# RWKV-7 / mLSTM trunk on one core: small products alternate between partition groups, and the state chain moves into one PSUM bank

## The chip, the core and the metric

The kernel runs on one core of a Trainium2 chip. The metric is the device time of one execution in microseconds, the median of several runs; lower is better. Engines are named as in the profile: PE (TensorE, matmuls), PEld (its weight loads), DVE (VectorE), ACT (ScalarE), POOL (GpSimd) and SP (SyncE, which issues most transfers).

## The reference, cut to what matters

Two layers over 1024 tokens of width 1024. Layer 0 mixes tokens with RWKV-7 (16 heads of 64) and layer 1 with a chunkwise mLSTM (8 heads); each is followed by a SwiGLU. What the change touches is mostly the RWKV-7 recurrence, one state of 64 x 64 for each head:

```
def _rwkv7_step(state, inp):
    r_t, w_t, k_t, v_t, a_t, b_t = inp
    sa = jnp.einsum('bhvk,bhk->bhv', state, a_t)
    state = state * w_t[:, :, None, :] + sa[..., None] * b_t[:, :, None, :] + v_t[..., None] * k_t[:, :, None, :]
    y = jnp.einsum('bhvk,bhk->bhv', state, r_t)
    return state, y
...
    w_log = -jax.nn.softplus(-(w0 + jnp.tanh(wl) @ w2)) - 0.5
    decay = jnp.exp(-jnp.exp(w_log.astype(jnp.float32)))
    a = jax.nn.sigmoid(a0 + al @ a2)
```

In the mLSTM it touches the scores inside a chunk, `jnp.einsum('bhctd,bhcsd->bhcts', q, k)`.

## The kernel before, in words

Activations lie with features on partitions and tokens along the free axis, in two halves of 512 tokens. A dense product is done in three passes (`dense`): weight and activation are each split into a high and a low part of type fp32r, and high x high, high x low and low x high are summed in one PSUM bank. These are the 128x512 matmuls named dn. A product of plain f32 operands is one call in the source and two MATMUL rows in the trace, so 256 calls stand there as x512.

RWKV-7 is computed in chunks of 64 tokens. A *pair* is two heads on the 128 partitions and one half of the tokens: 8 head pairs x 2 halves = 16 pairs, each of 8 chunks. Four functions work on a pair:

- `rw_prep` makes the chunk operands KB and AR and the scores: for each of two groups u and each head h, four products of 64 partitions (KB by AR) go into the one bank "sc", and two DVE multiplications by masks (line 630) write SA and SR from it.
- `rw_inverse` inverts the unit triangular 64 x 64 blocks in SA, starting with 16 x 16 blocks on DVE; then two rounds of 16 x 16 products (32 calls each, ordered by partition group q of 32 and then by chunk c) and, for e = 0 and then e = 1, two rounds of 32 x 32 products of 8 calls each. All use the one bank "iv", and ACT copies the result between rounds (lines 704, 712, 725, 729).
- `rw_solve` applies the inverse to the values (two rounds of 16 calls of 64 x 64 in bank "px") and to the chunk operand AR (for e = 0 and then e = 1, 8 calls in bank "tr").
- `rw_chain` carries the state through the 8 chunks, so 128 steps in all. A step: the product p1 = AR x state (bank "c1"), DVE adds p1 to VU (line 788), two products KT x VU into p3 (bank "c2"), DVE updates the state from p3 (line 793). Two products SR x VU, issued after the state update, are added into the other half of p1, and ACT copies that to Ys (line 798).

`chunks` runs 19 rounds: in round i the chain of pair i-3, the solve of pair i-2, the inverse of pair i-1, the prep of pair i and the finish of pair i-3. Between them it draws dense products from `fillers` (projections of the second half, gate, then the output projection and the first part of the SwiGLU) up to a quota. A list scheduler then sets the final order on every engine from this order and from priorities (`ahead`), each engine runs its instructions in that order, and the framework puts waits between accesses of different engines to one bank of the same PSUM tile. `bank(tag)` hands out a bank by tag: "dn" has two, each other tag one. The 8 banks are dn (2), sc, iv, tr, px, c1 and c2.

`lora` (the two low-rank maps for decay and a) adds a second product of 64 partitions, `hi[0:64] @ tl[0:64]`, to a first one of 128 partitions over `st`, whose upper half holds the high and whose lower half the low part of the same weights. It runs twice for each half of the tokens, with 8 output tiles each: 16 such products in each half. `ml_prep` computes for each of the 8 blocks of the mLSTM and for two heads four score products of 64 partitions, one head after the other, in banks "sc" and "iv".

Of the kernel before, what the change touches and what calls it, by code (L numbers as in the profile page):

```python
# [129 lines left out]
class K:  # L130
# [297 lines left out]
    def lora(self, hf, arr, xs=None):  # L428


        nc, A = self.nc, self.A
        first, second, bias, seg, func = {"s": ("lw", "w2", "w0", 1, AF.Tanh), "a": ("la", "a2", "a0", 4, AF.Copy)}[arr]
        xs = xs or self.mixed(seg)
        ps = self.bank("dn")
        self.dense(ps, self.weights(A[first]), xs)
        yield 5
        t = self.t("tmp")
        nc.scalar.activation(t, ps, func)
        th, tl = self.a0()
        self.split(th, tl, t)  # L440
        raw, hi, st = self.wtiles(A[second])
        nc.scalar.activation(hi, raw, AF.Copy)
        nc.scalar.activation(st[0:64], raw[0:64], AF.Copy)
        nc.vector.tensor_tensor(st[64:128], raw[64:128], hi[64:128].bitcast(F32), SUB)
        for j in range(KT):
            c = slice(j * P, j * P + P)
            ps = self.bank("dn")
            self.mm(ps, st[:, c], th, start=True, stop=False)
            self.mm(ps, hi[0:64, c], tl[0:64], start=False, stop=True)
            self.spill(arr, j, hf, ps, AF.Sigmoid, bias=self.col(bias, j))  # L450
            if hf == 0 or j % 4 == 3:
                yield 2
# [120 lines left out]
    def rw_prep(self, j, hf):  # L573
# [47 lines left out]
        for u in range(2):  # L621
            for h in range(2):
                hs = slice(64 * h, 64 * h + 64)
                ps = self.bank("sc", [P, 4, P])
                for q in range(4):
                    self.mm(ps[:, q], KB[hs, 4 * u + q, :], AR[hs, 4 * u + q, :])
                for t, at, m in ((SA, True, strict), (SR, False, incl)):
                    o = t.rearrange("p e (u h) t -> p u e h t", h=2)[:, 2 * u:2 * u + 2, :, h, :]
                    with self.ahead("mask"):
                        nc.vector.tensor_tensor(o, slots(ps, at), m, MUL)  # L630
# [26 lines left out]
    def rw_inverse(self, S):  # L657
# [39 lines left out]
        for q in range(4):  # L697
            r, e = slice(32 * q, 32 * q + 16), 0 if q >= 2 else 1
            o = 32 * (q % 2) + 16
            for c in range(8):  # L700
# [5 lines left out]
        for q in range(4):  # L706
            r = slice(32 * q, 32 * q + 16)
            for c in range(8):
# [10 lines left out]
        for e in range(2):  # L719
            o = 0 if e else 64  # L720
            r0, r1 = slice(o, o + 32), slice(o + 32, o + 64)
            ps = self.bank("iv", [P, 8, 32])
            for c in range(8):
                self.mm(ps[r1, c, :], SA[r0, e, c, 32:64], XN[r0, c, :], tile_position=(o, o + 32))
            nc.scalar.activation(Y1[r1], ps[r1], AF.Copy)
            ps = self.bank("iv", [P, 8, 32])
            for c in range(8):
                self.mm(ps[r0, c, :], Y1[r1, c, :], XD[r1, c, :], tile_position=(o + 32, o))
            nc.scalar.activation(SA[r0, e, :, 32:64], ps[r0], AF.Copy)

    def rw_solve(self, S):
# [22 lines left out]
        for c in range(8):  # L754
            vr, ur = self.rows(c)
            for h in range(2):
                o = (c // 2) * P + 64 * h
                self.mm(ps[ur, o:o + 64], SA[vr, c % 2, 2 * (c // 2) + h, :], VU[vr, c, 64 * h:64 * h + 64])
        nc.scalar.activation(Z, ps.rearrange("p (u f) -> p u f", f=P), AF.Copy)
        ps = self.bank("px")  # L760
        for c in range(8):
            vr, ur = self.rows(c)
            for h in range(2):
                o = (c // 2) * P + 64 * h
                self.mm(ps[ur, o:o + 64], SA[ur, c % 2, 2 * (c // 2) + h, :], Z[ur, c // 2, 64 * h:64 * h + 64])
        p3 = ps.rearrange("p (u f) -> p u f", f=P)
        nc.scalar.activation(VU[64:128, 0::2, :], p3[64:128], AF.Copy)
        nc.scalar.activation(VU[0:64, 1::2, :], p3[0:64], AF.Copy)
        for e in range(2):
            ps = self.bank("tr", [P, 4, 64])  # L770
            ur = self.rows(e)[1]
            for u in range(4):
                for h in range(2):
                    hs = slice(64 * h, 64 * h + 64)
                    self.mm(ps[hs, u, :], AT[ur, u, hs], SA[ur, e, 2 * u + h, :])
            nc.vector.tensor_copy(AR[:, e::2, ur], ps)
        S["VU"] = VU

    def rw_chain(self, S):
# [4 lines left out]
        for c in range(8):  # L784
            vr, ur = self.rows(c)
            p1 = self.bank("c1", [P, P])
            self.mm(p1, AR[:, c, :], st)
            nc.vector.tensor_tensor(VU[ur, c, :], p1[ur, :], VU[ur, c, :], ADD)
            p3 = self.p3
# [4 lines left out]
            for h in range(2):  # L794
                hs = slice(64 * h, 64 * h + 64)
                self.mm(p1[vr, hs], SR[:, c % 2, 2 * (c // 2) + h, :], VU[:, c, hs], start=False, stop=True,
                        skip_group_check=True)
# [486 lines left out]
    def ml_prep(self, pr, q, k, G):  # L1284
# [31 lines left out]
        for h in range(2):  # L1316
            w_ = dm[h].rearrange("p (c t) -> p c t", t=P)[:, :, P - 1:P]
            nc.vector.tensor_tensor(kw[:, :, 64 * h:64 * h + 64], p3[:, :, 64 * h:64 * h + 64],
                                    w_.to_broadcast([P, 4, 64]), MUL)
        for h in range(2):  # L1320
            hr = slice(64 * h, 64 * h + 64)
            ps = self.bank(self.alt("sc", "iv"))
            for c in range(4):
                cs = slice(c * P, c * P + P)
                self.mm(ps[:, cs], k[hr, cs], q[hr, cs])
            nc.vector.scalar_tensor_tensor(dm[h], ps, 0.125, dm[h], MUL, MUL)
# [182 lines left out]
    def build(self):  # L1509
# [66 lines left out]
        self.p3 = self.bank("c2", [P, P])  # L1576
        nc.vector.memset(self.p3, 0.0)
# [107 lines left out]
```

## Time and profile before

| | |
|---|---|
| time, median of 3 runs | 3062.93 us (3058.17 to 3084.75) |
| the profiled execution, its own time | 3071.16 us |
| its span in the trace | 3069.2 us |
| PE busy | 2875.5 us (94%) |
| DVE busy | 2041.1 us (67%) |
| ACT busy | 1409.5 us (46%) |
| mean granted TensorE clock | 0.919 |

The span is what the trace shows from the first to the last instruction; the execution's own time has about 2 us around it. Busy time is a union of intervals, and since matmuls overlap in the array, a busy PE is not PE at its peak. The RWKV-7 rounds lie between about 219 and 1130 us, the mLSTM between about 2000 and 2290 us.

### The profile page before, as it was taken

What the parts mean: (1) busy time and instruction counts of PE and PEld (TensorE: products, weight loads), DVE (VectorE), ACT (ScalarE), POOL (GpSimd) and SP (SyncE); (2) the same over time, 40 slices, a digit from 0 to 9 for tenths busy, and PEclk for the clock granted to TensorE, in tenths of its full rate; (3) what the DMA queues carried; (4) which work ended last, traced back from release to release, by engine and by line L of the source; (5) the groups of instructions that cost most, each with busy time, mean ns of one, the idle gap of its engine ahead of it and who ended that gap; (6) DMA issues with size and microseconds to landing.
All of it is one profiled execution on the core that took longest, in us unless ns stands there. A gap on an engine that the chain in (4) does not pass through costs nothing.

```text
span 3069.2 us, 46769 instructions
## 1 busy us (share of the span) xinstructions
PE 2875.5 (94%) x17080; PEld 2254.1 (73%) x17080; DVE 2041.1 (67%) x4029; ACT 1409.5 (46%) x2641; POOL 73.5 (2%) x98
## 2 busy tenths in 40 slices
PE   6799989999989898999999998999989999999998
PEld 5577657677767677788877776777857788887776
DVE  7866665757666545978887758755555766667645
ACT  5756665656655554532224335322344533332532
POOL 0000000000000000000000000000010000000000
PEclk9899767979979689999999999988989999999999
DMA  8774433435354236466778854344545233336734
GB/s 289 258 236 141 111 98 92 116 101 142 102 155 125 80 95 210 151 191 220 239 243 281 270 178 157 115 124 151 158 134 168 93 117 103 103 114 229 256 120 149
DMA packets 359721, 492.38 MB, mean 160 GB/s; under 512 B 125212, under 2 KB 208796, under 8 KB 359492
## 3 DMA queue, kind: packets, MB, share of 16 engines
q1 hardware_dynamic: 345668, 464.24, 47.9%
q10 hardware_dynamic: 13824, 25.17, 2.2%
q8 instruction: 134, 2.20, 0.3%
q14 instruction: 95, 0.78, 0.1%
HBM read 359.77 MB, written 129.50 MB: 159 GB/s over the span
## 4 chain that ended last, share of the span: by engine, by line
PE 61%; DVE 13%; DMA 12%; issue 7%; ACT 5%; POOL 1%; SPq 1%; DVEq 0%; POOLq 0%; ACTq 0%
PE dn L207 23%; PE c L207 18%; PE iv L207 8%; PE px L207 6%; PE sc L207 4%; DMA tt<-gd 2%; DMA wraw<-in_wdn 2%; DMA wraw<-wsd 1%; DMA bgs<-in_ada 1%; DVE wq L212 1%; ACT wq L211 1%; DVE ga L212 1%; PE tr L207 1%; DMA bgs<-in_wdn 1%; DMA wsd<-bgs 1%
## 5 line engine op out<-in xcount | busy, mean ns | idle before, releaser
L207 PE MATMUL dn<-a,whi 128*128 128x512 f32 (+1 forms) x1224 | 473.2, 451 | 19.1 <-ACT a L211 7.8
L207 PE MATMUL c<-ga,wq 128*128 128x512 f32 x1446 | 355.6, 395 | 10.2 <-ACT ga L211 8.6
L211 ACT ACTIVATE wq<-wraw 128x1024 fp32r<-128x1024 f32 x202 | 210.7, 1057 | 330.9 <-DVE wraw L890 82.0
L207 PEld LDWEIGHTS c<-ga,wq 128*128 128x128 f32 x1446 | 271.9, 190 | 76.2 <-ACT ga L211 11.5
L207 PEld LDWEIGHTS dn<-a,whi 128*128 128x128 f32 (+1 forms) x1224 | 242.8, 206 | 89.4 <-issue 14.6
L212 DVE TENSOR_TENSOR wq<-wraw,wq 128x1024 fp32r<-128x1024 f32 x202 | 244.3, 1221 | 85.1 <-ACT wq L211 84.8
L207 PE MATMUL dn<-a,wlo 128*128 128x512 f32 (+2 forms) x640 | 284.1, 448 | 7.6 <-ACT tmp L420 3.0
L207 PE MATMUL c<-gb,wq 128*128 128x512 f32 x894 | 221.6, 399 | 7.6 <-DVE wq L212 6.9
L207 PEld LDWEIGHTS c<-gb,wq 128*128 128x128 f32 x894 | 169.5, 192 | 47.9 <-DVE wq L212 8.0
L207 PEld LDWEIGHTS dn<-a,wlo 128*128 128x128 f32 (+2 forms) x640 | 131.3, 206 | 40.2 <-issue 6.8
L211 ACT ACTIVATE whi<-wraw 128x1024 fp32r<-128x1024 f32 (+2 forms) x96 | 100.4, 1046 | 127.4 <-PE dn L207 104.1
L212 DVE TENSOR_TENSOR wlo<-wraw,whi 128x1024 fp32r<-128x1024 f32 (+2 forms) x96 | 116.1, 1209 | 48.4 <-ACT whi L211 41.3
L207 PE MATMUL iv<-ga,wq 128*128 128x512 f32 x552 | 136.0, 389 | 0.0
L207 PE MATMUL px<-ga,wq 128*128 128x512 f32 x528 | 128.6, 389 | 0.0
L207 PEld LDWEIGHTS iv<-ga,wq 128*128 128x128 f32 x552 | 103.6, 188 | 21.5
L211 ACT ACTIVATE w<-wraw 128x384 fp32r<-128x384 f32 (+1 forms) x100 | 56.7, 567 | 129.6 <-PE c L207 55.0
L207 PEld LDWEIGHTS px<-ga,wq 128*128 128x128 f32 x528 | 99.1, 188 | 20.7
L207 PE MATMUL dn<-gb,wq 128*128 128x512 f32 x426 | 104.7, 397 | 5.2 <-ACT gb L211 4.7
L207 PE MATMUL iv<-gb,wq 128*128 128x512 f32 x432 | 104.9, 390 | 0.0
L207 PEld LDWEIGHTS dn<-gb,wq 128*128 128x128 f32 x426 | 81.3, 192 | 24.5 <-ACT gb L211 5.6
L207 PEld LDWEIGHTS sc<-AR,KB 64*128 64x128 f32 x512 | 77.9, 226 | 28.5 <-issue 14.0
L207 PE MATMUL sc<-AR,KB 64*128 64x128 f32 x512 | 94.6, 331 | 3.9 <-DVE KB L612 3.2
(600 smaller groups left out, 5761.7 us busy)
## 6 DMA issues: line engine op xcount, KB each, us to landing
wraw<-in_wgu SPq DMA_DIRECT2D x110, 512.0 KB, 3.6
tt<-gd SPq DMA_DIRECT2D x154, 256.0 KB, 4.0
KT<-in_ada SPq DMA_DIRECT2D x40, 512.0 KB, 5.4
gd<-x SPq DMA_DIRECT2D x77, 256.0 KB, 2.1
gd<-tt SPq DMA_DIRECT2D x72, 256.0 KB, 2.2
wraw<-wsd SPq DMA_DIRECT2D x32, 512.0 KB, 4.5
bgs<-in_ada SPq DMA_DIRECT2D x96, 128.0 KB, 3.4
wraw<-in_wdn SPq DMA_DIRECT2D x24, 512.0 KB, 4.4
```

The costliest lines, as they stand in the source:

```text
L207: return self.nc.tensor.matmul(out, lhsT, rhs, start=start, stop=stop, **kw)
L211: self.nc.scalar.activation(hi, src, AF.Copy)
L212: self.nc.vector.tensor_tensor(lo, src, hi.bitcast(F32), SUB)
```

## The change

1. `lora`: the second product takes all 128 partitions of `st` and `tl` (it adds low x low).
2. `rw_prep`: both heads of a group are issued alternately, head 0 into bank "sc" and head 1 into bank "c1"; the mask multiplications follow.
3. `rw_inverse`: the 16 x 16 products run over c outside and q inside; the 32 x 32 rounds of e = 0 and e = 1 are done together, one allocation of "iv" for each round.
4. `rw_solve`: the products are listed so that each call takes another partition group than the one before; the last round is done for e = 0 and 1 together, in banks "tr" and "px".
5. `rw_chain`: p1 moves out of "c1" into two slots of p3's own bank "c2", and the two SR products are issued before the two KT products.
6. `ml_prep`: both heads' scores are issued alternately, in "sc" and "iv".

```diff
-            self.mm(ps, hi[0:64, c], tl[0:64], start=False, stop=True)
+            self.mm(ps, st[:, c], tl, start=False, stop=True)
...
         for u in range(2):
+            ps = [self.bank(tag, [P, 4, P]) for tag in ("sc", "c1")]
+            for q in range(4):
+                for h in range(2):
+                    hs = slice(64 * h, 64 * h + 64)
+                    self.mm(ps[h][:, q], KB[hs, 4 * u + q, :], AR[hs, 4 * u + q, :])
             for h in range(2):
-                hs = slice(64 * h, 64 * h + 64)
-                ps = self.bank("sc", [P, 4, P])
-                for q in range(4):
-                    self.mm(ps[:, q], KB[hs, 4 * u + q, :], AR[hs, 4 * u + q, :])
...
-        for q in range(4):
-            r, e = slice(32 * q, 32 * q + 16), 0 if q >= 2 else 1
-            o = 32 * (q % 2) + 16
-            for c in range(8):
+        for c in range(8):
+            for q in range(4):
+                r, e = slice(32 * q, 32 * q + 16), 0 if q >= 2 else 1
+                o = 32 * (q % 2) + 16
                 self.mm(ps[r, c, :], SA[r, e, c, o:o + 16], XN[r, c, 0:16], tile_position=(32 * q, 32 * q))
...
-        for e in range(2):
-            o = 0 if e else 64
-            r0, r1 = slice(o, o + 32), slice(o + 32, o + 64)
-            ps = self.bank("iv", [P, 8, 32])
-            for c in range(8):
+        ends = [(e, o, slice(o, o + 32), slice(o + 32, o + 64)) for e, o in enumerate((64, 0))]
+        ps = self.bank("iv", [P, 8, 32])
+        for c in range(8):
+            for e, o, r0, r1 in ends:
                 self.mm(ps[r1, c, :], SA[r0, e, c, 32:64], XN[r0, c, :], tile_position=(o, o + 32))
+        for e, o, r0, r1 in ends:
             nc.scalar.activation(Y1[r1], ps[r1], AF.Copy)
-            ps = self.bank("iv", [P, 8, 32])
-            for c in range(8):
+        ps = self.bank("iv", [P, 8, 32])
+        for c in range(8):
+            for e, o, r0, r1 in ends:
                 self.mm(ps[r0, c, :], Y1[r1, c, :], XD[r1, c, :], tile_position=(o + 32, o))
+        for e, o, r0, r1 in ends:
             nc.scalar.activation(SA[r0, e, :, 32:64], ps[r0], AF.Copy)
...
-        for c in range(8):
-            vr, ur = self.rows(c)
-            for h in range(2):
-                o = (c // 2) * P + 64 * h
-                self.mm(ps[ur, o:o + 64], SA[vr, c % 2, 2 * (c // 2) + h, :], VU[vr, c, 64 * h:64 * h + 64])
+        pairs = [(2 * u + e, h, u * P + 64 * h, *self.rows(e)) for u in range(4) for h in range(2) for e in range(2)]
+        for c, h, o, vr, ur in pairs:
+            self.mm(ps[ur, o:o + 64], SA[vr, c % 2, 2 * (c // 2) + h, :], VU[vr, c, 64 * h:64 * h + 64])
...
+        ps = [self.bank(tag, [P, 4, 64]) for tag in ("tr", "px")]
+        for u in range(4):
+            for h in range(2):
+                hs = slice(64 * h, 64 * h + 64)
+                for e in range(2):
+                    ur = self.rows(e)[1]
+                    self.mm(ps[e][hs, u, :], AT[ur, u, hs], SA[ur, e, 2 * u + h, :])
         for e in range(2):
-            ps = self.bank("tr", [P, 4, 64])
-            ur = self.rows(e)[1]
-            for u in range(4):
-                for h in range(2):
-                    hs = slice(64 * h, 64 * h + 64)
-                    self.mm(ps[hs, u, :], AT[ur, u, hs], SA[ur, e, 2 * u + h, :])
-            nc.vector.tensor_copy(AR[:, e::2, ur], ps)
+            nc.vector.tensor_copy(AR[:, e::2, self.rows(e)[1]], ps[e])
...
-            p1 = self.bank("c1", [P, P])
+            p1 = self.p3[:, 1 + c % 2]
             self.mm(p1, AR[:, c, :], st)
             nc.vector.tensor_tensor(VU[ur, c, :], p1[ur, :], VU[ur, c, :], ADD)
-            p3 = self.p3
+            p3 = self.p3[:, 0]
+            for h in range(2):
+                hs = slice(64 * h, 64 * h + 64)
+                self.mm(p1[vr, hs], SR[:, c % 2, 2 * (c // 2) + h, :], VU[:, c, hs], start=False, stop=True,
+                        skip_group_check=True)
             for h in range(2):
                 hs = slice(64 * h, 64 * h + 64)
                 self.mm(p3[hs, hs], KT_[:, c, hs], VU[:, c, hs])
             nc.vector.scalar_tensor_tensor(st, st, dl[:, c:c + 1], p3, MUL, ADD)
-            for h in range(2):
-                hs = slice(64 * h, 64 * h + 64)
-                self.mm(p1[vr, hs], SR[:, c % 2, 2 * (c // 2) + h, :], VU[:, c, hs], start=False, stop=True,
-                        skip_group_check=True)
...
+        ps = [self.bank(tag) for tag in ("sc", "iv")]
+        for c in range(4):
+            cs = slice(c * P, c * P + P)
+            for h in range(2):
+                hr = slice(64 * h, 64 * h + 64)
+                self.mm(ps[h][:, cs], k[hr, cs], q[hr, cs])
         for h in range(2):
-            hr = slice(64 * h, 64 * h + 64)
-            ps = self.bank(self.alt("sc", "iv"))
-            for c in range(4):
-                cs = slice(c * P, c * P + P)
-                self.mm(ps[:, cs], k[hr, cs], q[hr, cs])
-            nc.vector.scalar_tensor_tensor(dm[h], ps, 0.125, dm[h], MUL, MUL)
+            nc.vector.scalar_tensor_tensor(dm[h], ps[h], 0.125, dm[h], MUL, MUL)
...
-        self.p3 = self.bank("c2", [P, P])
-        nc.vector.memset(self.p3, 0.0)
+        self.p3 = self.bank("c2", [P, 3, P])
+        nc.vector.memset(self.p3[:, 0], 0.0)
```

Two places in the order on PE follow; a row is a line of the source, the operation, the tile it writes and those it reads. First the scores of one pair with a step of the chain between them, before (sc is the bank of the scores, c_302 is p3, c_1283 is p1 and dn a dense product):

```order
L207 MATMUL sc_6916<-AR_6903,KB_6902 128x128 [waits DVE_49]
L207 MATMUL sc_6916<-AR_6903,KB_6902 128x128 x3
L207 MATMUL px_6953<-pt_6949,br_6951 128x512 [waits DVE_49]
L207 MATMUL c_302_1589<-VU_6564,KT_5756 64x64 [waits DVE_49]
L207 MATMUL c_302_1589<-VU_6564,KT_5756 64x64
L207 MATMUL c_1283_7056<-VU_6564,SR_5711 64x64 x2
L207 MATMUL dn_6979<-a_5822,whi_6975 128x512
L207 MATMUL dn_6979<-a_5821,wlo_6976 128x512
L207 MATMUL dn_7181<-a_7122,whi_7177 128x512
L207 MATMUL sc_6923<-AR_6903,KB_6902 128x128 [waits DVE_49,PE_49]
L207 MATMUL sc_6923<-AR_6903,KB_6902 128x128 x3
```

and the same place now (c_1184 is the second head's bank, c_302 holds p1 and p3):

```order
L207 MATMUL sc_6842<-AR_6829,KB_6828 128x128 [waits DVE_49]
L207 MATMUL c_1184_6843<-AR_6829,KB_6828 128x128
L207 MATMUL sc_6842<-AR_6829,KB_6828 128x128
L207 MATMUL c_1184_6843<-AR_6829,KB_6828 128x128
L207 MATMUL sc_6842<-AR_6829,KB_6828 128x128
L207 MATMUL c_1184_6843<-AR_6829,KB_6828 128x128
L207 MATMUL sc_6842<-AR_6829,KB_6828 128x128
L207 MATMUL c_1184_6843<-AR_6829,KB_6828 128x128
L207 MATMUL c_302_1589<-VU_6492,SR_5657 64x64 [waits DVE_49]
L207 MATMUL c_302_1589<-VU_6492,SR_5657 64x64
L207 MATMUL c_302_1589<-VU_6492,KT_5702 64x64 x2
```

Four groups of four calls for a pair have become two groups of eight that change heads at every call, and SR now stands ahead of KT.

The second place is one whole step of the chain between dense products on PE, before:

```order
L207 MATMUL c_1288_7101<-st_1582,AR_5699 128x128 [waits DVE_49,Activation_49]
L207 MATMUL dn_7468<-a_7158,whi_7464 128x512
L207 MATMUL dn_7181<-a_7164,whi_7177 128x512 [waits Activation_49]
L207 MATMUL iv_6819<-XD_6718,Y_1232_6808 32x32 [waits DMAHW3_49,Activation_49]
L207 MATMUL iv_6819<-XD_6718,Y_1232_6808 32x32 x7
L207 MATMUL c_302_1589<-VU_6564,KT_5756 64x64 [waits DVE_49]
L207 MATMUL c_302_1589<-VU_6564,KT_5756 64x64
L207 MATMUL c_1288_7101<-VU_6564,SR_5711 64x64 x2
L207 MATMUL dn_7468<-a_7157,wlo_7465 128x512
L207 MATMUL dn_7181<-a_7165,whi_7177 128x512 [waits DVE_49]
```

and one now:

```order
L207 MATMUL c_302_1589<-st_1582,AR_5645 128x128 [waits Activation_49]
L207 MATMUL dn_7384<-a_7055,whi_7380 128x512
L207 MATMUL dn_7384<-a_7054,wlo_7381 128x512
L207 MATMUL dn_7384<-a_7061,whi_7380 128x512
L207 MATMUL dn_7099<-a_7083,whi_7095 128x512 [waits DVE_49]
L207 MATMUL c_302_1589<-VU_6492,SR_5657 64x64 [waits DVE_49]
L207 MATMUL c_302_1589<-VU_6492,SR_5657 64x64
L207 MATMUL c_302_1589<-VU_6492,KT_5702 64x64 x2
L207 MATMUL dn_7099<-a_7082,wlo_7096 128x512
L207 MATMUL dn_7099<-a_7089,whi_7095 128x512 [waits Activation_49]
```

The step's first product waited for DVE (the state update) and for ACT (the copy of the step before); it now waits for ACT alone. What ACT waits for shows in its own order, where Ys is the copy of a step's output and whi a weight split. Before:

```order
L798 ACTIVATE Ys_6455<-c_1194_6456 64x128 [waits DVE_49,PE_49]
L211 ACTIVATE whi_6851<-wraw_6849 128x1024 [waits DMAHW6_49,PE_49]
L420 ACTIVATE tmp_6559<-dn_6534 128x512 [waits PE_49]
L798 ACTIVATE Ys_6455<-c_1195_6465 64x128 [waits DVE_49,PE_49]
```

Here the copy waited for the VU addition on DVE and for SR on PE. On ACT now, at the pair's chain:

```order
L797 ACTIVATE Ys_6391<-c_302_1589 64x128 [waits DVE_49]
L809 ACTIVATE gj_6354,gv_6353<-Ys_5844,gm_6352 128x64 [waits Activation_49]
L211 ACTIVATE whi_6568<-wraw_6566 128x1024 [waits DMAHW4_49]
L809 ACTIVATE gj_6354,gv_6353<-Ys_5844,gm_6352 128x64 [waits Activation_49] x3
L797 ACTIVATE Ys_6391<-c_302_1589 64x128 [waits DVE_49]
```

The copy has moved behind the state update on DVE of its own step, and the next step's first product stands behind the copy.

## Rows read from the trace of the kernel before

**Rows 1.** The page: span, granted TensorE clock in 40 slices, chain of waits by engine.

```profile
span 3069.2 us, 46769 instructions
...
PEclk9899767979979689999999999988989999999999
...
PE 61%; DVE 13%; DMA 12%; issue 7%; ACT 5%; POOL 1%; SPq 1%; DVEq 0%; POOLq 0%; ACTq 0%
```

**Rows 2.** Busy time by stage: the RWKV-7 rounds and the mLSTM.

```profile
core 0: us, PE busy (x) PEld busy (x) DVE busy (x) ACT busy (x) POOL busy (x), PEclk, DMA share, GB/s
...
219.00:1130.00 911.00, 864.78 (x7979) 638.04 (x7978) 564.99 (x1453) 540.24 (x1256) 30.26 (x31) 0.82 0.41 115
...
2000.00:2290.00 290.00, 269.75 (x1518) 218.65 (x1517) 161.94 (x449) 101.35 (x243) 23.07 (x32) 0.91 0.43 136
```

**Rows 3.** Groups of PE, 219 to 1130 us: busy us, mean ns | idle before, releaser.

```profile
L207 PE MATMUL dn<-a,whi 128*128 128x512 f32 x768 | 305.6, 458 | 8.0 <-DVE a L212 3.5 <-ACT a L211 1.8 <-ACT tmp L420 1.7
...
L207 PE MATMUL sc<-AR,KB 64*128 64x128 f32 x512 | 94.6, 331 | 3.9 <-DVE KB L612 3.2 <-DVE Y L675 0.4
...
L207 PE MATMUL tr<-SA,AT 64*64 64x64 f32 x512 | 32.0, 251 | 5.2 <-DVE AR L776 3.7 <-ACT AT L751 1.5
L207 PE MATMUL px<-VU,SA 64*64 64x64 f32 x512 | 31.6, 248 | 0.1
L207 PE MATMUL iv<-XN,SA 32*32 32x32 f32 x512 | 30.1, 223 | 2.0 <-DVE X L677 1.2 <-DVE XN L713 0.8
L207 PE MATMUL iv<-XD,Y 32*32 32x32 f32 x512 | 29.8, 222 | 1.4 <-ACT Y L725 1.4
L207 PE MATMUL px<-Z,SA 64*64 64x64 f32 x512 | 26.5, 250 | 0.5 <-ACT SA L729 0.5
...
L207 PE MATMUL iv<-XB,Y 16*16 16x16 f32 x1024 | 25.2, 176 | 1.1 <-ACT Y L704 0.7
L207 PE MATMUL iv<-XN,SA 16*16 16x16 f32 x1024 | 24.6, 173 | 0.0
...
L207 PE MATMUL dn<-a,whi 64*128 64x512 f32 x16 | 11.3, 734 | 0.0
```

**Rows 4.** Timeline of PE, one block's mLSTM scores: start us, us, what, xcount.

```profile
2006.36 0.42 PE L207 MATMUL sc<-x,x 64*128 64x128 f32 x1
2006.54 0.42 PE L207 MATMUL iv<-x,x 64*128 64x128 f32 x1
2006.57 0.42 PE L207 MATMUL sc<-x,x 64*128 64x128 f32 x1
2006.75 0.42 PE L207 MATMUL iv<-x,x 64*128 64x128 f32 x1
```

**Rows 5.** Timeline of PE around 700 us, at full clock.

```profile
700.00 1.16 PE L207 MATMUL sc<-AR,KB 64*128 64x128 f32 x8
701.08 1.12 PE L207 MATMUL px<-pt,br 128*128 128x512 f32 x2
...
715.80 1.52 PE L207 MATMUL iv<-XN,SA 16*16 16x16 f32 x64
717.25 0.55 PE L818 MATMUL tr<-kc,Ys 128*128 128x128 f32 x3
...
721.62 0.40 PE L207 MATMUL c<-VU,SR 128*64 128x64 f32 x4
721.95 0.50 PE L207 MATMUL dn<-a,wlo 128*128 128x512 f32 x1
```

**Rows 6.** Timeline of PE, a solve's second round in bank px.

```profile
857.05 1.20 PE L207 MATMUL px<-Z,SA 64*64 64x64 f32 x32
858.03 0.28 PE L207 MATMUL tr<-SA,AT 64*64 64x64 f32 x2
```

**Rows 7.** Groups of DVE and ACT, 219 to 1130 us, columns as in rows 3.

```profile
L793 DVE SCALAR_TENSOR_TENSOR st<-st,dl,c 128x128 f32<-128x128 f32 x122 | 41.8, 343 | 48.4 <-PE c L207 47.1
...
L420 ACT ACTIVATE tmp<-dn 128x512 f32<-128x512 f32 x46 | 26.9, 589 | 7.6 <-PE dn L207 7.2 <-ACT Ys L798 0.2
...
L798 ACT ACTIVATE Ys<-c 64x128 f32<-64x128 f32 x121 | 32.8, 271 | 83.6 <-PE c L207 82.0
```

**Rows 8.** Waits of PE, 219 to 1130 us: us in total, times, longest us.

```profile
PE c L207 <- DVE VU L788: 4.4, 10, 0.9
...
PE c L207 <- DVE st L793: 1.5, 2, 1.4
```

More of the change, by code (lines that the diff above doesn't have):

```diff
@@ L629, in rw_prep @@
                     with self.ahead("mask"):
-                        nc.vector.tensor_tensor(o, slots(ps, at), m, MUL)
+                        nc.vector.tensor_tensor(o, slots(ps[h], at), m, MUL)
         d0 = self.dram.tile([2, 2, 8, 32, 32], F32, tag="d0", name=self.nm("d0"), bufs=4)
@@ L705, in rw_inverse @@
         ps = self.bank("iv", [P, 8, 16])
-        for q in range(4):
-            r = slice(32 * q, 32 * q + 16)
-            for c in range(8):
+        for c in range(8):
+            for q in range(4):
+                r = slice(32 * q, 32 * q + 16)
                 self.mm(ps[r, c, :], Y1[r, c, 0:16], XB[r, c, :], tile_position=(32 * q, 32 * q))
@@ L718, in rw_inverse @@
         Y1 = self.t("Y1", [P, 8, 32])
-        for e in range(2):
-            o = 0 if e else 64
-            r0, r1 = slice(o, o + 32), slice(o + 32, o + 64)
-            ps = self.bank("iv", [P, 8, 32])
-            for c in range(8):
+        ends = [(e, o, slice(o, o + 32), slice(o + 32, o + 64)) for e, o in enumerate((64, 0))]
+        ps = self.bank("iv", [P, 8, 32])
+        for c in range(8):
+            for e, o, r0, r1 in ends:
                 self.mm(ps[r1, c, :], SA[r0, e, c, 32:64], XN[r0, c, :], tile_position=(o, o + 32))
+        for e, o, r0, r1 in ends:
             nc.scalar.activation(Y1[r1], ps[r1], AF.Copy)
-            ps = self.bank("iv", [P, 8, 32])
-            for c in range(8):
+        ps = self.bank("iv", [P, 8, 32])
+        for c in range(8):
+            for e, o, r0, r1 in ends:
                 self.mm(ps[r0, c, :], Y1[r1, c, :], XD[r1, c, :], tile_position=(o + 32, o))
+        for e, o, r0, r1 in ends:
             nc.scalar.activation(SA[r0, e, :, 32:64], ps[r0], AF.Copy)
@@ L753, in rw_solve @@
         ps = self.bank("px")
-        for c in range(8):
-            vr, ur = self.rows(c)
-            for h in range(2):
-                o = (c // 2) * P + 64 * h
-                self.mm(ps[ur, o:o + 64], SA[vr, c % 2, 2 * (c // 2) + h, :], VU[vr, c, 64 * h:64 * h + 64])
+        pairs = [(2 * u + e, h, u * P + 64 * h, *self.rows(e)) for u in range(4) for h in range(2) for e in range(2)]
+        for c, h, o, vr, ur in pairs:
+            self.mm(ps[ur, o:o + 64], SA[vr, c % 2, 2 * (c // 2) + h, :], VU[vr, c, 64 * h:64 * h + 64])
         nc.scalar.activation(Z, ps.rearrange("p (u f) -> p u f", f=P), AF.Copy)
         ps = self.bank("px")
-        for c in range(8):
-            vr, ur = self.rows(c)
-            for h in range(2):
-                o = (c // 2) * P + 64 * h
-                self.mm(ps[ur, o:o + 64], SA[ur, c % 2, 2 * (c // 2) + h, :], Z[ur, c // 2, 64 * h:64 * h + 64])
+        for c, h, o, vr, ur in pairs:
+            self.mm(ps[ur, o:o + 64], SA[ur, c % 2, 2 * (c // 2) + h, :], Z[ur, c // 2, 64 * h:64 * h + 64])
         p3 = ps.rearrange("p (u f) -> p u f", f=P)
@@ L793, in rw_chain @@
             nc.vector.scalar_tensor_tensor(st, st, dl[:, c:c + 1], p3, MUL, ADD)
-            for h in range(2):
-                hs = slice(64 * h, 64 * h + 64)
-                self.mm(p1[vr, hs], SR[:, c % 2, 2 * (c // 2) + h, :], VU[:, c, hs], start=False, stop=True,
-                        skip_group_check=True)
             nc.scalar.activation(Ys[vr, c // 2, :], p1[vr, :], AF.Copy)
```

## The prediction

> **What bounds the kernel now.** I read the page first: the chain of waits is 61% PE, and the clock line dips only in a stretch early on [rows 1]. Busy time by stage shows where: in the RWKV-7 rounds, 911 us of the span, PE is busy for 864.78 us (46 us idle), and its mean granted clock is 0.82 [rows 2]. The clock has two levels, 1.2 and 2.4 GHz; a mean of 0.82 says that about 36% of the stage, 328 us, ran at the lower one. DVE is busy for 565 and ACT for 540 us there, so PE is the bound of this stage, and the change is read from there. The groups of PE show what it does: besides the dense products, small ones [rows 3]. PE itself seldom waits for the state chain: 4.4 us for VU, 1.5 us for the state [rows 8].
>
> **What two small products cost when they stand in different partition groups.** The mLSTM scores show it by accident. There both heads stood in the queue, head 0 in bank sc and head 1 in iv, and the trace has them side by side: sc starts at 2006.36 and 2006.57, iv at 2006.54 and 2006.75 [rows 4]. Each head keeps its own step of 0.21 us, as if the other weren't there. So two heads in turns, in two banks, should cost PE what one costs.
>
> **The change part by part.** All savings are PE time in its own stage.
>
> Scores of `rw_prep`: 512 rows, 94.6 us [rows 3], in 64 groups of 8 (16 pairs, 2 groups u, 2 heads): 1.48 us a group on average, and 1.08 us at full clock from its start to the next kind's [rows 5]. Afterwards there are 32 groups of 16 rows, each as long as one head's: 32 x 1.48 = -47 us. The ends: 0 if nothing overlaps, -47 if all does; the mLSTM rows are the same form, so I take -47.
>
> 16 x 16 products: 24.6 + 25.2 = 49.8 us [rows 3], 64 rows in 1.45 us, 23 ns each [rows 5]. They go tile after tile now. Four tiles in turns give between -25 (two at once) and -37 us (four at once), 0 if none; no row shows four, so I take -27, near two.
>
> 32 x 32 products: 30.1 + 29.8 = 59.9 us [rows 3] in four groups a pair, one tile each. Two tiles in turns halve that: -30; I take -28, since the groups that remain still have a lead-in. ACT's copies between the rounds come as four rounds before and two after, which shortens the inverse but isn't on the path that ends the stage.
>
> Solve: the last round, tr, takes 32.0 us [rows 3]; its two heads are two column groups already, and e adds a second pair: between 0 and -16, I take -8. The two px rounds already change partition groups at every second call. 32 rows take 0.98 us, 31 ns each [rows 6], against 0.33 us for four SR rows of 64 columns in one column group [rows 5]: the queue has found the overlap by itself. So 31.6 + 26.5 us keep most of their length: between 0 and -10, I take -3.
>
> The Trainium skill has a rule that speaks against the inverse and the px rounds: "TensorEngine Tiling (Array Packing)", section "Restrictions and Gotchas", says that different row tiles cannot access the same PSUM bank at the same time. By that rule iv and px would gain nothing. The px rows above lie in one bank and overlap all the same, so the trace disagrees, where the partitions written differ too.
>
> `lora`: the product of 64 partitions takes 734 ns on average, a dense one of the same width 458 [rows 3]; 16 x 0.276 = 4.4 us in the stage, and as many products ahead of it: I take -6 (between 0 and -9).
>
> `ml_prep`: 8 blocks x 2 heads x 8 rows at the lengths of the RWKV scores are 16 x 1.2 = 19 us. Half goes at most, and one block overlaps already [rows 4]: -7 (0 to -9).
>
> Together: -(47 + 27 + 28 + 8 + 3 + 6 + 7) = -126 us, out of a stage of 911 and a little outside it.
>
> The chain: a step went product, VU, KT, state, product; SR and the copy to Ys stood beside the state update. Now SR stands ahead of KT, and the copy lies between the state update and the next product. That adds a copy of 0.271 us [rows 7] and about 0.2 us for four SR rows: 0.47 x 128 steps = 60 us if nothing lies beside it. The waiting instruction is PE's first product of a step, and everything on PE is queued behind it; on ACT the copy waits for DVE and holds up the weight splits behind it. The cover is the two to four dense products that the order puts between KT and the next product. They hid nearly all of the old latency [rows 8], and nothing shows how much is left over; between 0 and +60, I take a third: +20 us.
>
> Lost cover: the small products were themselves cover for DVE's and ACT's answers. PE idles for 46 us of the stage [rows 2]. With 126 us less to do at the same distances some answers come late: between 0 and half of it, +63; I take a quarter, +30 us.
>
> Clock: the 328 us at the lower level go with stretches of small products. If they shrink with the stage (126 of 911, 14%), 45 us of low clock go, each worth half: -23 us. It could be three times as much, -70, if the small products are what pulls the clock down, or +30 if a PE that idles more is granted less. I take -23.
>
> The sum is -126 + 20 + 30 - 23 = -99 us, made against the profiled execution's 3071 us (span 3069.2 and some 2 us around it): 2972. That execution lies 8 us above the median of the runs shown, 3063, so on their scale it is 2964 us, 3.2% faster.
>
> **Rivals.**
> - *The cover is the bound.* PE has less to do, but DVE, ACT and the chain answer no sooner: half of the saving is idle time (+63), the chain costs +50, the clock gives nothing. -126 + 63 + 50 = -13 us: 3050. For it: ACT waits 82.0 us on PE for Ys already, so the copy is seldom ready at once [rows 7]. Against it: PE hardly waits now [rows 8].
> - *Tiles that share a bank don't overlap.* Then only the scores, `lora` and the mLSTM gain, -(47 + 6 + 7) = -60, with +20 for the chain, +15 for lost cover and -10 from the clock: -35, so 3028 us. The skill's rule above would give this; rows 6 speak against it, rows 4 have two banks. The near neighbour is that the queue overtakes so well that new orders bring nothing (px): the scores can't be that case, for a head waited for the bank of the other.
> - *The ring through ACT decides.* Every step then pays the copy (0.271), SR (0.2) and, in front of the copy, one other ACT instruction such as an eviction of 0.589 us [rows 7]: 1.06 x 128 = +136 us. With -126 saved and +30 of lost cover that is +40: 3103 us, slower. It outweighs the gain from about 70% of the price on, (126 - 30) / 136. For it: ACT is busy 59% of the stage. Against it: most steps have room between KT and the next product, and a step lasts 7 us on average (911 / 128).
>
> **How the numbers follow.** The forecast, 2964 us, has a chance of 0.78; its own range, from the terms' ends, is 2895 to 3030. The covered case has 0.10, the shared bank 0.06, the ring 0.06. The range that should hold 8 in 10 reaches from 2895 (all small products at their best and twice the clock's gain) to 3035, where the shared bank is in it and the covered case is left out. A measurement can tell about 1% (31 us) from no change. Faster by over 1%, below 3032: 0.78 less a little, most of the shared bank and a part of the covered case, 0.84. Within 1%: 0.10. Slower: 0.06, the ring.
>
> **What would show it.** Right: sc and the second bank start in turns and the RWKV scores fall from 94.6 to about 48 us; the 16 x 16 groups from 49.8 to 23, the 32 x 32 from 59.9 to 32; the stage from 911 to about 815 us, with a granted clock of 0.82 or more. Wrong: sc at 90 us or more together with the second bank; PE idle over 110 us in the stage, with the state chain or ACT's Ys as releaser of c; a step's first product waiting for ACT by more than 0.5 us at most steps; a clock below 0.78.

## The result and the profile after

The changed kernel takes 2923.82 us (median of four runs, 2919.56 to 2926.81) against 3064.2 us in four runs before: a ratio of 0.953 [0.949, 0.957]. The forecast was 2964 us, range 2895 to 3035. The profiled execution took 2919.56 us, against 3071.16 before and 2972 in the sum.

First the page of the changed kernel: span, busy time, granted clock, chain by engine.

```profile
span 2917.8 us, 46574 instructions
...
PE 2702.9 (93%) x17080; PEld 2124.4 (73%) x17080; DVE 2036.1 (70%) x4029; ACT 1401.1 (48%) x2641; POOL 74.5 (3%) x98
...
PEclk9899789999798999999999989889989999999999
...
PE 61%; DVE 14%; DMA 11%; ACT 6%; issue 6%; POOL 1%; SPq 1%; DVEq 0%; POOLq 0%; ACTq 0%
```

PE still carries 61% of the chain [rows 1], and the early dip of the clock is shallower. To compare like with like I take the stage from the first RWKV score to the first SwiGLU product of the same pass. Its two rows, before and then after (us from span start; length; busy; granted clock; DMA):

```profile
219.40:1174.00 954.60, 901.55 (x8168) 665.07 (x8167) 583.63 (x1487) 559.42 (x1305) 31.90 (x32) 0.83 0.41 117
```

```profile
211.50:1025.80 814.30, 736.18 (x8168) 536.05 (x8167) 581.78 (x1490) 553.87 (x1309) 33.74 (x32) 0.92 0.47 136
```

The stage lost 140 us, the time ahead of it 8 and that behind it 3. PE runs as many rows (8168) in 165 us less; DVE and ACT have as much to do as before. PE's idle time went from 53 to 78 us. The clock went from 0.83 to 0.92: with two levels, the lower half the upper, the stage spent 2 x 0.17 x 954.6 = 325 us at the lower one before and 2 x 0.08 x 814.3 = 130 us now. The granted clock is given to 0.01 there; its records in the two traces add up to 334 and 137 us, and these are used below.

Groups of PE in that stage, by form (busy us, mean ns | idle before, releaser):

```profile
L207 PE MATMUL dn<-a,whi 128*128 128x512 f32 x848 | 312.7, 431 | 9.3 <-DVE a L212 4.0 <-ACT a L211 2.1 <-ACT tmp L420 1.0
...
L207 PE MATMUL c<-VU,KT 128*64 128x64 f32 x512 | 63.5, 244 | 0.0
L207 PE MATMUL c<-VU,SR 128*64 128x64 f32 x512 | 61.3, 243 | 5.8 <-DVE VU L787 5.5
L207 PE MATMUL c<-st,AR 128*128 128x128 f32 x256 | 60.1, 319 | 10.1 <-ACT Ys L797 7.9 <-DVE AR L775 1.6
L207 PE MATMUL c<-AR,KB 64*128 64x128 f32 x256 | 45.9, 318 | 0.0
L207 PE MATMUL sc<-AR,KB 64*128 64x128 f32 x256 | 44.9, 317 | 9.1 <-DVE SR L631 3.8 <-DVE KB L612 3.4 <-DVE AR L613 1.8
...
L207 PE MATMUL iv<-XD,Y 32*32 32x32 f32 x512 | 13.3, 209 | 6.4 <-ACT Y L726 6.4
L207 PE MATMUL iv<-XN,SA 32*32 32x32 f32 x512 | 13.0, 204 | 6.6 <-DVE XN L714 5.0 <-DVE X L678 1.1 <-DVE Y L676 0.2
...
L207 PE MATMUL iv<-XB,Y 16*16 16x16 f32 x1024 | 11.2, 177 | 0.9 <-ACT Y L705 0.5
L207 PE MATMUL iv<-XN,SA 16*16 16x16 f32 x1024 | 11.1, 176 | 1.6 <-DVE XN L695 1.6
```

Against [rows 3]: a single row is hardly shorter (318 ns for 331, 176 for 173, 209 for 222), but the union is half or less: 22.3 us for the 16 x 16 products (49.8), 26.3 for the 32 x 32 (59.9). The two score groups, 44.9 and 45.9 us, are one stretch lying in both banks, against 94.6. Some waits have grown: iv on ACT's Y from 1.4 to 6.4 us, c on Ys from 0.7 to 7.9 us.

The timeline of PE in the changed kernel shows the turns (start us, us, what, count):

```profile
524.70 0.37 PE L207 MATMUL sc<-AR,KB 64*128 64x128 f32 x1 [1.83 <-DVE AR L613]
524.71 0.37 PE L207 MATMUL c<-AR,KB 64*128 64x128 f32 x1
524.92 0.27 PE L207 MATMUL sc<-AR,KB 64*128 64x128 f32 x1
524.92 0.27 PE L207 MATMUL c<-AR,KB 64*128 64x128 f32 x1
...
525.59 0.27 PE L207 MATMUL sc<-AR,KB 64*128 64x128 f32 x1
525.59 0.27 PE L207 MATMUL c<-AR,KB 64*128 64x128 f32 x1
...
555.43 0.69 PE L207 MATMUL iv<-XN,SA 16*16 16x16 f32 x64
556.05 0.27 PE L207 MATMUL c<-VU,SR 128*64 128x64 f32 x1
556.06 0.27 PE L207 MATMUL c<-VU,KT 128*64 128x64 f32 x1
556.15 0.22 PE L207 MATMUL c<-VU,SR 128*64 128x64 f32 x1
556.17 0.22 PE L207 MATMUL c<-VU,KT 128*64 128x64 f32 x1
556.21 0.28 PE L207 MATMUL c<-VU,SR 128*64 128x64 f32 x2
556.33 0.28 PE L207 MATMUL c<-VU,KT 128*64 128x64 f32 x2
556.54 0.50 PE L207 MATMUL dn<-a,whi 128*128 128x512 f32 x1
```

The sixteen score rows of both heads take 1.16 us (524.70 to 525.86), which is what eight took before [rows 5]. 64 rows of 16 x 16 take 0.62 us (555.43 to 556.05) instead of 1.45 [rows 5]: the four tiles overlap, in one bank. SR and KT start side by side too, but that shortens nothing: their eight rows in a step take 0.49 us (556.05 to 556.54), and before, KT and then SR took 0.50 (713.12 to 713.62). A step before:

```profile
713.12 0.34 PE L207 MATMUL c<-VU,KT 128*64 128x64 f32 x4
713.29 0.40 PE L207 MATMUL c<-VU,SR 128*64 128x64 f32 x4
713.50 0.35 DVE L793 SCALAR_TENSOR_TENSOR st<-st,dl,c 128x128 f32<-128x128 f32 x1 [0.75 <-PE c L207]
713.62 0.50 PE L207 MATMUL dn<-a,whi 128*128 128x512 f32 x1
713.85 0.27 ACT L798 ACTIVATE Ys<-c 64x128 f32<-64x128 f32 x1
```

and the state update and the copy of the step shown above, now:

```profile
556.65 0.35 DVE L796 SCALAR_TENSOR_TENSOR st<-st,dl,c 128x128 f32<-128x128 f32 x1 [0.55 <-PE c L207]
557.33 0.27 ACT L797 ACTIVATE Ys<-c 64x128 f32<-64x128 f32 x1
```

The state update starts 0.60 us after the first of the eight rows, where it was 0.38; over all 128 steps these are the shortest distances of each kernel.

Adding up, over all PE records of the stage, the distance from each row's start to the next one's (so idle time counts with the row ahead of it) gives a sum that closes:

| kind of row | before | after | difference |
|---|---|---|---|
| scores | 91.4 | 50.6 | -40.8 |
| 16 x 16 | 47.6 | 22.1 | -25.5 |
| 32 x 32 | 58.4 | 31.9 | -26.5 |
| solve | 80.0 | 69.8 | -10.2 |
| chain (AR x state, SR, KT) | 138.0 | 123.1 | -14.9 |
| dense (dn) | 450.5 | 429.5 | -21.0 |
| transposes and the rest | 88.8 | 87.3 | -1.5 |
| stage | 954.7 | 814.3 | -140.4 |

The groups that were put in turns (the first four lines) bring -103 us. The rest, -37, comes from rows whose number hardly changed; the forecast's terms for what isn't a small product's own length (+20, +30, -23) came to +27.

### The profile page after: what moved, and what is told of

It is laid out like the page before. It is cut to its first block, busy times and chain, and to the rows that moved or that the text cites. A ratio compares the mean times of both kernels' runs of the same rounds, so it can differ in the third digit from the quotient of the medians.

```text
span 2917.8 us, 46574 instructions
## 1 busy us (share of the span) xinstructions
PE 2702.9 (93%) x17080; PEld 2124.4 (73%) x17080; DVE 2036.1 (70%) x4029; ACT 1401.1 (48%) x2641; POOL 74.5 (3%) x98
## 4 chain that ended last, share of the span: by engine, by line
PE 61%; DVE 14%; DMA 11%; ACT 6%; issue 6%; POOL 1%; SPq 1%; DVEq 0%; POOLq 0%; ACTq 0%
PE dn L207 23%; PE c L207 20%; PE iv L207 7%; PE px L207 7%; PE sc L207 2%; DMA wraw<-wsd 2%; DMA tt<-gd 1%; DMA wraw<-in_wdn 1%; DVE wq L212 1%; DMA bgs<-in_ada 1%; DVE ga L212 1%; ACT wq L211 1%; DVE wlo L212 1%; PE tr L207 1%; ACT whi L211 1%
## 5 line engine op out<-in xcount | busy, mean ns | idle before, releaser
L207 PE MATMUL dn<-a,whi 128*128 128x512 f32 (+1 forms) x1200 | 434.4, 428 | 20.4 <-ACT a L211 8.0
L207 PEld LDWEIGHTS dn<-a,whi 128*128 128x128 f32 (+1 forms) x1200 | 226.3, 196 | 81.8 <-ACT a L211 10.7
L207 PE MATMUL dn<-a,wlo 128*128 128x512 f32 (+1 forms) x664 | 275.1, 425 | 5.8 <-ACT wlo L443 2.9
L207 PEld LDWEIGHTS dn<-a,wlo 128*128 128x128 f32 (+1 forms) x664 | 128.8, 197 | 37.1 <-issue 4.8
L207 PE MATMUL iv<-ga,wq 128*128 128x512 f32 x552 | 136.0, 389 | 0.0
L207 PE MATMUL c<-ga,w 128*128 128x512 f32 x372 | 93.4, 393 | 1.1 <-DVE ga L212 0.7
L1124 ACT ACTIVATE x<-x 128x512 f32<-128x512 f32 x77 | 48.3, 629 | 95.0 <-DVE x L933 44.9
```

The source lines that it names most:

```text
L207: return self.nc.tensor.matmul(out, lhsT, rhs, start=start, stop=stop, **kw)
L1124: nc.scalar.activation(t, t, AF.Silu)
```

## The experiments

My theory: the time left where small products stand side by side, and with each of their microseconds some low clock went too, which made the dense and chain rows shorter. Rivals: the reordered chain itself gave or cost time; the freed bank mattered and not the turns; the order as a whole came out better by luck.

Differences between two kernels below are those of their ratios, on 3064 us; since each ratio is known to 0.002 to 0.004, they are good to about 14 us. Low-clock time is added up from the granted clock's records in each trace, over the stage cut as above. Every edit also lets the scheduler find another order, so a difference holds whatever that moved as well.

**1. Scores as before** (one bank, head after head).

```diff
-            ps = [self.bank(tag, [P, 4, P]) for tag in ("sc", "c1")]
...
             for h in range(2):
+                hs = slice(64 * h, 64 * h + 64)
+                ps = self.bank("sc", [P, 4, P])
...
```

> The changed kernel, with the RWKV scores as before (one bank, head after head). If two heads at once are what the scores gain, their rows go back from 50.6 to about 91 us and the time to 2965 to 2980 us (41 us of rows and some low clock with them). If the bank's round trip and not PE time had been the gain, the rows come back but PE fills the gaps, and the time stays within 10 us of 2924. Granted clock in the RWKV rounds: 0.88 to 0.92 by the first.

Measured: 2980.62 us, 0.970 [0.968, 0.972], so +52 us over the changed kernel. The score rows are back at 90.8 us (+40) and the clock is at 0.88:

```profile
211.40:1074.50 863.10, 792.52 (x8169) 579.67 (x8168) 584.11 (x1490) 559.63 (x1309) 34.70 (x32) 0.88 0.45 129
```

The rows came back and the time with them, to the upper edge of the forecast. The second bank and the turns together are worth their rows and some 30% more.

**2. Scores and chain as before**: also p1 in "c1", KT ahead of SR.

```diff
-            p1 = self.p3[:, 1 + c % 2]
+            p1 = self.bank("c1", [P, P])
...
```

> As the run with the scores as before, and the chain as before too (own bank for its first product, SR after KT). The difference of the two is the price of the new chain alone. By the prediction it costs 20 us, so this run is 20 us faster than the other. A rival: the copy to Ys is covered and SR beside KT saves a change of products, so this run is 5 to 15 us slower. A third: no difference, within 5 us.

Measured: 2981.4 us, 0.971 [0.967, 0.974], the same as run 1, and the chain's rows take 136.0 us against 134.9. That is the third forecast. With the same scores, the old and the new chain cost the same, to within some 12 us: a price of 20 us is excluded, and a gain of that size too.

**3. Inverse as before** (q outside, c inside; e = 0 and then e = 1).

```diff
-        for c in range(8):
-            for q in range(4):
+        for q in range(4):
...
+            for c in range(8):
...
```

> The changed kernel with the inverse as before. Theory: the long stretches of 16 x 16 and 32 x 32 products are what brings the low clock; with them back the granted clock of the RWKV rounds falls from 0.92 to 0.86 or less, and the time rises by 52 us of rows and 30 to 50 of clock, to 3005 to 3030 us. Rival: the clock follows all small products alike; it falls to about 0.89, and the time to 2970 to 2990 us.

Measured: 3000.06 us, 0.975 [0.972, 0.978], +68 us, for 50 us of rows more (55.1 + 49.0 against 31.9 + 22.1); the clock is 0.87. It is the largest part of those taken away. Time and clock lie between the two forecasts, so the run doesn't say whether the products of the inverse pull the clock down more than other small ones.

**4. Two banks, but head by head**: keeps the bank for each head and takes the turns away.

```diff
-            for q in range(4):
-                for h in range(2):
+            for h in range(2):
+                for q in range(4):
```

> The changed kernel with the scores in two banks, but all four calls of head 0 ahead of the four of head 1. If the queue overtakes far enough by itself (as the mLSTM rows showed late in a group), two banks are most of the gain: 2924 to 2935 us. If calls must alternate, head 0's first calls run alone: half to all of the scores' gain is lost, 2945 to 2970 us.

Measured: 2943.12 us, 0.958 [0.954, 0.961]: +15, not told apart from zero by the time alone, but the score rows take 72.7 us, halfway between 50.6 and 91.4. The timeline of PE in this run:

```profile
214.13 0.82 PE L207 MATMUL sc<-AR,KB 64*128 64x128 f32 x5
214.68 0.37 PE L207 MATMUL c<-AR,KB 64*128 64x128 f32 x1
214.79 0.27 PE L207 MATMUL sc<-AR,KB 64*128 64x128 f32 x1
...
215.12 0.72 PE L207 MATMUL c<-AR,KB 64*128 64x128 f32 x5
```

The second head starts only when some four of the first head's eight rows are through, overlaps the others, and runs its last five rows alone. So of the gain in rows the bank gives about one half and the turns the other. The time lies between the two forecast ranges.

**5. Solve as before.**

```diff
...
-        ps = [self.bank(tag, [P, 4, 64]) for tag in ("tr", "px")]
...
         for e in range(2):
+            ps = self.bank("tr", [P, 4, 64])
```

> The changed kernel with the solve as before. Its rows go back from 70 to 80 us. If PE's rows decide, the time is 8 to 18 us above 2924 (2932 to 2942). Rival: the queue finds the overlap of the solve by itself and the rest is hidden: within 6 us.

Measured: 2939.07 us, 0.958 [0.956, 0.960], +15, but the solve's rows take 70.5 us with the old order and 69.8 with the new. The forecast 80 did not come: the edit gives these rows nothing. Nearly all of the 10 us that they lost against before lie in the clock: where rows of one form are compared at its two levels, the solve's have 12.5 us of extra time at the lower one before and 3.2 in the changed kernel. Where the 15 us come from, if they are there, stays open.

**6. `lora` as before, and 7. `lora` alone** (the kernel before, with this line new: the edit below the other way round).

```diff
-            self.mm(ps, st[:, c], tl, start=False, stop=True)
+            self.mm(ps, hi[0:64, c], tl[0:64], start=False, stop=True)
```

> The changed kernel with the product of 64 partitions back in lora. If its 32 products cost 0.2 to 0.4 us more each on PE's path, the time rises by 6 to 13 us, and the first RWKV score starts some 4 to 8 us later than 211.5 us. Rival: other engines bound the first half, and only the 16 products inside the rounds count: 0 to 5 us.

> The kernel before with lora's second product over 128 partitions and nothing else. Undoing it in the changed kernel cost 30 us, where its rows account for some 12. If that was the product itself and the clock around it, the time falls here by 20 to 35 us too. If it was the order that the scheduler happened to find, it falls by 5 to 15 us.

Measured: taken back, 2954.19 us, 0.964 [0.962, 0.967], +35; alone, 3044.38 us, 0.992 [0.989, 0.994], -25. The row of PE in the run that takes it back, over the same stage:

```profile
L207 PE MATMUL dn<-a,whi 64*128 64x512 f32 x16 | 10.6, 674 | 0.0
```

674 ns against 431 for a full dense row makes 16 x 0.24 = 4 us, as the forecast had it, and the stage starts at 216.8 us, 5.3 later, as it had it too. But the +35 lie far above the 6 to 13 us that were forecast from the rows. Alone the edit moves the start of the stage from 219.4 to 209.7 us and shortens the stage by 18.6, with dense rows of 438.2 us for 450.5. The sixteen rows don't explain that; which neighbours gain isn't settled.

**8. The old chain, with the second head's scores in "px".** The bank c1 stays with the chain.

```diff
-            ps = [self.bank(tag, [P, 4, P]) for tag in ("sc", "c1")]
+            ps = [self.bank(tag, [P, 4, P]) for tag in ("sc", "px")]
...
+            p1 = self.bank("c1", [P, P])
```

> The changed kernel with the chain as before, and the scores in turns in banks sc and px (c1 stays with the chain). If the chain's new form serves only to free a bank and px has room, the time is that of the changed kernel, 2918 to 2932 us. If px is too busy (solve and two broadcasts for each pair lie in it), the scores wait for it and 10 to 30 us are lost: 2935 to 2955 us.

Measured: 2933.73 us, 0.956 [0.954, 0.958], +10, not told apart from the changed kernel. As far as 14 us can tell, what the new chain does is free a bank, and another one would have done.

**9. The new inverse alone** (in the kernel before).

```diff
...
-            for c in range(8):
+        for c in range(8):
+            for q in range(4):
...
```

> The kernel before, with the inverse of the changed one and nothing else. Its rows fall from 106 to about 54 us. If a microsecond of small products is worth what the runs so far show (1.3 to 1.4 us of time, 1.6 to 1.8 us of low clock), the time falls by 65 to 75 us to some 2990 to 3000, and low-clock time from 334 to about 245 us. Rival: the clock needs the scores shortened too; then only rows count, 45 to 55 us, 3010 to 3020, and the low-clock time stays above 290 us.

Measured: 2989.9 us, 0.973 [0.971, 0.976], -82 us for 51 us of rows (106.0 to 55.2). The clock of the stage is 0.89 where it was 0.83, with the chain and the dense products in their old form; low-clock time fell from 334 to 191 us. Both go beyond the forecast of 65 to 75 us and 245 us.

**10. Each 16 x 16 product issued twice** (the same values are written twice).

```diff
+                for _ in range(2):
...
+                for _ in range(2):
```

> The changed kernel with each of the 16 x 16 products issued twice (the second overwrites the first). Their rows go from 22 to about 44 us. If stretches of small products bring the low clock, the low-clock time of the RWKV rounds rises from 137 us by 35 us or more (as in the runs with scores or inverse as before, 1.6 to 1.8 us for each us of rows), and the time by 30 to 45 us, more than the rows themselves: 2954 to 2969 us. Rival: the rows alone count, +15 to +25 us, and low-clock time stays below 155 us.

Measured: 2987.17 us, 0.975 [0.972, 0.977], +66 us. The stage and its two 16 x 16 groups:

```profile
210.60:1086.40 875.80, 787.12 (x10216) 575.61 (x10215) 584.72 (x1490) 559.57 (x1309) 33.20 (x32) 0.87 0.45 127
```

```profile
L207 PE MATMUL iv<-XB,Y 16*16 16x16 f32 x2048 | 24.2, 180 | 27.2 <-issue 23.0 <-ACT Y L706 4.0
...
L207 PE MATMUL iv<-XN,SA 16*16 16x16 f32 x2048 | 20.8, 174 | 0.9 <-issue 0.9
```

Twice the rows are 45.0 us busy where one set took 22.3, so the overlap holds; but 23 us of "issue" are counted with them, in which PE waits for no other engine. By distances they went from 22.1 to 71.4. This idle time lies inside the second 16 x 16 round of a pair and not ahead of it: in 15 of the 16 rounds PE stops once, for 0.1 to 4.1 us, and each stop ends 1.2 to 1.6 us after a transfer of 16 KB on the DMA queue called "instruction" has landed. The run has 150 such transfers, the changed kernel 134, and there no such stop shows. So PE seems to wait for its own instructions.

The time and the rows went beyond the forecast (30 to 45 us, and 44 us of rows), and low-clock time rose from 137 to 223 us. But about as much idle time was added as small rows, and the run doesn't tell which of the two cost the clock. It agrees with the theory and is no clean test of it.

**11. Four dense products ahead of each 16 x 16 round** (their result isn't used).

```diff
+        t = self.bank("iv")
+        for _ in range(4):
+            self.mm(t, self.iv[:, 0:P], self.iv)
...
-        ps = self.bank("iv", [P, 8, 16])
+        ps, fill = self.filled()
...
```

> The changed kernel with four dense products of 112 partitions and 512 columns, whose result is overwritten or never read, ahead of each of the two 16 x 16 rounds: 128 products of about 0.23 us, 29 us of PE time. If low clock follows from stretches with little dense work, this raises the granted clock: low-clock time falls from 137 to 110 us or less, and the time rises by less than the products' own 29 us (0 to 20 us). Rival: low-clock time stays or grows, and the time rises by 25 to 45 us.

Measured: 2949.18 us, 0.960 [0.957, 0.963], +22 us, although the added rows are busy for 44.6 us:

```profile
210.30:1040.30 830.00, 760.64 (x8296) 551.10 (x8295) 582.97 (x1490) 560.20 (x1311) 31.00 (x32) 0.94 0.47 134
```

In the profile the stage grew by 16 us. The clock rose from 0.92 to 0.94 and the kernel's own dense rows went from 429.5 to 413.1. Low-clock time fell from 137 to 103 us, as forecast; the time rose a little more than the 20 us. So over half of the added rows' time came back in the stage. At most 17 us of it can be clock (34 us less at the lower level, each worth up to half); PE's idle time fell by 9 us, and the rest isn't settled. As a remedy it still loses.

**12. Broadcasts over the full height**: the 40 products of 48 partitions that spread a row over the partitions take 112, with zeros. It was meant to beat the changed kernel.

```diff
-        rows = slice(64 * hf, 64 * hf + 48)
...
-        self.mm(ps, sel.rearrange("p h d -> p (h d)"), self.iv[rows])
+        self.mm(ps, sel.rearrange("p h d -> p (h d)"), self.iv)
```

> The changed kernel, with its 40 broadcasts of 48 partitions (16 in the RWKV rounds, 24 in the mLSTM) over 112 partitions, the rest zeros in the selector; the selectors are made by one DVE addition of two slices of the identity. As with lora, a product that leaves partitions out is the suspect: each takes 0.42 us here and holds up the one before it by 0.1 us, where a dense one of 512 columns takes 0.23. If that is what lora gained by, 40 x 0.29 = 12 us go, and some low clock: 8 to 20 us below the changed kernel, at a ratio of 0.946 to 0.950 to the kernel before. Rival: they stand alone between other forms and are off PE's path: ratio 0.952 to 0.956.

Measured: 2955.79 us, 0.963 [0.960, 0.966], about 1% slower than the changed kernel, outside both forecasts. The broadcasts' rows took 482 ns instead of 513 in the stage, 0.5 us over 15 of them; the waits of the chain's first product grew:

```profile
L207 PE MATMUL c<-st,AR 128*128 128x128 f32 x256 | 61.2, 324 | 15.4 <-ACT Ys L797 13.3 <-DVE AR L775 1.6
```

The chain's rows went from 123.1 to 141.1 us, though nothing in the chain was edited. Shortening rows isn't enough where the chain's answers come closer to the products that wait for them. No run beat the changed kernel, and in none of the twelve were the chain's rows as short: 126.8 to 141.1 us. A part of its gain may be a lucky order.

## Why the prediction was right, and where it was off

**The bound and the overlap were right.** The scores lost 40.8 us (the sum had 47), the 16 x 16 rows 25.5 (27), the 32 x 32 rows 26.5 (28). Scores at 45 to 46 us, 22.3 and 26.3 us of busy time and a clock of 0.92 are what the forecast named as its signs. The stage of [rows 2], to come down from 911 to about 815 us, went further, to 771 for as many rows:

```profile
219.00:990.00 771.00, 702.27 (x7979) 510.06 (x7978) 559.04 (x1445) 533.94 (x1261) 32.10 (x31) 0.91 0.47 133
```

For the 16 x 16 I took "near two" tiles at once; with four the groups fell further, and waits gave part of that back. Runs 1, 3 and 9 each show such a part to be worth time by itself, in both directions.

**The chain's +20 us was mis-sized: about nothing was paid.** The latencies that the sum put in line are there. SR holds the state update up by 0.22 us at the least (0.60 against 0.38), and the copy ends 0.37 us after the state update at the median, where it was 0.15. What was wrong is the share that comes through, "I take a third": run 2 against run 1 puts the price at 2 us, give or take 12. The dense products between the steps hid nearly all of it, since PE waits for the copy only nine times in 128 steps. PE's waits in the stage of the changed kernel (total us, times, longest):

```profile
PE c L207 <- ACT Ys L797: 7.9, 9, 4.5
PE iv L207 <- ACT Y L726: 6.4, 8, 1.1
PE c L207 <- DVE VU L787: 5.5, 8, 1.3
```

For the chain that is 13.4 us together, where before VU, the state update and the copy had 6.6 in the same stage (4.4, 1.5 and 0.7). The ring through ACT, the rival with the slower end, thus exists and decides nothing.

**The clock's -23 us was the term that was mis-sized.** I let the low clock shrink with the stage, 14%; it shrank by 59%, 334 to 137 us. Each of these microseconds is worth up to half of one, so up to 99 us. Comparing rows of one form at the two levels gives 139 us of extra time before and 51 after, -88; that lies beyond the end of -70 which I had kept for "the small products are what pulls the clock down". Some 34 of the -88 are inside the small rows' own -103; the sum had priced these rows at their mean length, low clock included, so its clock term counted that part again. The rest is in the dense, chain and other rows (-21, -15 and -2 by distances, for waits took part of it back).

Runs 1 and 3 give 52 us of time for 40 of rows and 68 for 50, and run 9 gives 82 for 51: 1.3 to 1.6 us for each us of small rows, each ratio good to some 0.3. The whole change has 140 for 103. That the surplus runs through the clock is supported by the same comparison of rows (77 us of extra time in run 1 and 88 in run 3, against 51) and by run 11, which moved the clock with dense rows put ahead of the small ones. No run holds the clock still, so what it is in stretches of small products that brings the lower level stays open.

**Smaller terms.** `lora`, -6: alone it gave -25, ahead of the stage and inside it, and the price of its 32 rows, taken as 0.24 us each, explains some 8 of these. The solve, -8 and -3: nothing by run 5. `ml_prep`, -7: everything behind the stage lost 3 us, so no more than that shows; it wasn't tried apart.

**Lost cover, +30,** was about right: PE's idle time rose by 25 us, the chain's share in it.

**Rivals.** The covered case needed idle time of half the saving; it was about a sixth. A shared bank does not keep tiles from overlapping where they write other partitions: 64 rows in the one bank iv take 0.62 us. The Trainium skill, "TensorEngine Tiling (Array Packing)", section "Restrictions and Gotchas", has it that different row tiles can't access one PSUM bank at the same time; here the trace disagrees, as [rows 6] had said before. That the queue overtakes by itself is half true, as run 4 shows.

**The range.** Its lower end, 2895 us, doesn't follow from the terms: with all small products at their best (-158) and twice the clock's gain (-46), and the other two as they stand, the sum gives 2909. The result, 2924, lies in the range either way.

## What to carry to other kernels

Where small products stand in other partition groups, issue them in turns and give each head or group its own place to write: the queue finds only a part of the overlap by itself (72.7 us, against 50.6 in turns). Read the granted clock of the stage beside the busy time; where it is low and small products fill the stage, time taken from them was worth 1.3 to 1.6 times itself here. A reordered dependent chain is priced from the waits that the profile shows at it, and not from the length of what was put in line; and judge a part by a run with and without it and not by its rows alone, since `lora` alone brought three times what its own rows cost.

## What the runs showed of the hardware

- SR and KT write one bank (c2) and start side by side all the same, but their eight rows take 0.49 us, where one after the other they took 0.50.
- With two banks and one head after the other in the queue, the second head's rows started ahead of the first head's last three (run 4).
- With each 16 x 16 product issued twice, PE stopped inside 15 of 16 rounds, 23.0 us in all, each time until 1.2 to 1.6 us after a 16 KB transfer of the "instruction" queue had landed.
- A product of 64 partitions and 512 columns among full ones took 674 to 734 ns, the full ones 431 to 458.
- Four dense products ahead of a round of 16 x 16 ones raised the stage's granted clock from 0.92 to 0.94, and the stage grew by 16 us for their 44.6.
